# Attention of a hybrid encoder: products with v once per head over 512 queries, in place of twice over 256

## The chip, the cores and the metric

The kernel runs on one core of a Trainium2 chip. The metric is the device time of one execution in microseconds (us); a version's time is the median of its runs. A core has five engines that work side by side, each through its own queue in order: TensorE (PE in the profile; its weight loads are PEld), VectorE (DVE), ScalarE (ACT), GpSimd (POOL) and SyncE (SP, which here only issues DMAs). They wait for each other by semaphores.

## The reference

The model has two layers over 512 tokens of 1024 features in float32: a gated linear attention with a gated MLP, then a softmax attention with a second MLP. The change lies in the softmax attention. It has 8 query heads of 128 features; heads 0 to 3 share the first key and value head, 4 to 7 the second. Cut to what matters:

```python
def block(q_blk):                       # 128 queries
    s = jnp.einsum('bkgqd,bksd->bkgqs', q_blk, k).astype(jnp.float32) * scale
    p = jax.nn.softmax(s, axis=-1).astype(v.dtype)
    return jnp.einsum('bkgqs,bksd->bkgqd', p, v)

o = lax.map(block, qb)                  # 4 blocks of 128 queries
return o @ w_out                        # after the heads are put side by side
```

q and k have been normalised and rotated before. So each head gives, for each of its 512 queries, a row of 512 probabilities times v.

## The kernel before, in words

All products run in a reduced float32 form (fp32r). To keep the accuracy, each operand is split into a high part and a low part (the remainder), and each product is done as three: high by high, high by low, low by high (`mm3`, lines 266 to 268, which is where the profile puts them). A split is one copy on ScalarE (the high part) and one subtraction on VectorE (the low part).

The attention (`attention`, from line 640) first makes k, the first pair of q heads and v. `vh` and `vl` hold v, split, as four tiles of 128 tokens by 256 features. Then comes a loop that is written out by hand, over 32 blocks (8 heads times 4 blocks of 128 queries) and six steps more. Step t does, in this order of the program:

- `scores` of block t: three products of 512 columns into a PSUM bank "s" (two banks), the row maximum (`mx`, line 785), its scaling (`nb`, 786), and the exponential on ScalarE with the row sums (`p`, 788).
- what the plan gives for step t: steps of the q projections of the heads still to come (banks A and B, 24 products for each of the two banks, rotary products `rt` at line 679, splits of q), and from step 22 on steps of the output projection (`op`, line 321).
- `turn` of block t-4: four transposes of 128 x 128 into a bank "pt" (two banks, line 806), then the split of the transposed probabilities: `pth` (line 809, ScalarE) and `ptl` (line 810, VectorE), each 128 x 512.
- `shares` of block t: the reciprocal of the sum (`rc`, 793) and the scaling of p (794).
- `mix`, on every second step: the products with v for half a head (block t-6 and the one before). It takes four tiles of v times three products, each with 256 columns, the two blocks of queries, into one half of the bank "po" (one bank). After the second half the bank is split into oT (lines 705 and 706), which the output projection reads.

A half's transposed probabilities are one tile pair from the pool "g" (22 tiles), laid out as four key tiles by 256 queries. oT comes from "g" for heads 0 to 3 and from the pool "xhl" (8 tiles) for heads 4 to 7; "xhl" also holds the normalised input of the next MLP (`Norm.chunk`, lines 231 to 244), made in pairs of 128-feature chunks as the output projection ends. A scheduler orders the program's instructions for each engine by its own estimate of their times and keeps the program's order only where data demand it, so the order on each queue can shift when the program changes.

At the start, line 178 on, seven small float32 products on constants ("warm", each of which the profile records as two) run before the first data arrive. Their sum, -0.5, is copied to `halfneg` (line 184), the exponent of the reciprocal square roots later. The first real products are those of `vg` (line 295); their weights are the normalised x, their moving operand the first weights w_vg, split into `wh` and `wl`.

After the attention come the second MLP's up-products (`up`) and down-products (`dn`) with the same `mm3`.

Of the kernel before, what the change touches and what calls it, by code (L numbers as in the profile page):

```python
# [8 lines left out]
F32 = mybir.dt.float32  # L9
F32R = mybir.dt.float32r  # L10
U8 = mybir.dt.uint8
AF = mybir.ActivationFunctionType
ALU = mybir.AluOpType

P = 128
S = 512
D = 1024
KC = D // P
NT = S // P
# [27 lines left out]
def hybrid_encoder_kernel(  # L47
# [21 lines left out]
    pe, act, dve, pool, sync = nc.tensor, nc.scalar, nc.vector, nc.gpsimd, nc.sync  # L69
    mm = pe.matmul  # L70
# [7 lines left out]
    def nm(s):  # L78
        uid[0] += 1
        return f"{s}{uid[0]}"  # L80
# [3 lines left out]
    def bank(tag, n):  # L84
        return pp.tile([P, S], F32, tag=tag, bufs=PS[tag], name=nm(n))

    def pair(tag, bufs, dt, n):
        return sp.tile([P, 2 * S], dt, tag=tag, bufs=bufs, name=nm(n))

    def big(dt, n):  # L90
        return pair("g", 22, dt, n)

    def tmp(tag, n, w=S):
        return sp.tile([P, w], F32, tag=tag, bufs={"u": 4, "t": 6, "sq": 3}[tag], name=nm(n))
# [81 lines left out]

    two = tmp("u", "two")
    dve.memset(two[:, :P], 2.0 ** -5)
    dve.memset(two[:, P : 2 * P], -(2.0 ** -5))
    warm = bank("po", "warm")  # L180
    for i in range(7):
        mm(warm[:, :P], two[:, :P], two[:, P : 2 * P], start=i in (0, 3), stop=i in (2, 6))
    halfneg = cp.tile([P, 8], F32, name="halfneg")
    dve.tensor_copy(halfneg, warm[:, :8])
    ones = cp.tile([P, 1], F32, name="ones")
# [78 lines left out]
    def mm3(ps, wh, wl, mh, ml, start, stop):  # L264

        mm(ps, wh, mh, start=start, stop=False)  # L266
        mm(ps, wh, ml, start=False, stop=False)  # L267
        mm(ps, wl, mh, start=False, stop=stop)  # L268
# [371 lines left out]
    def attention(norm, nxt):  # L640
# [63 lines left out]
        def split(y, tile_):  # L704
            act.activation(tile_[:, :S], y, AF.Copy)
            dve.tensor_tensor(tile_[:, S:], y, tile_[:, :S].bitcast(F32), ALU.subtract)

        def whole(gen):
            while True:
                try:  # L710
                    next(gen)
                except StopIteration as e:
                    return e.value
# [52 lines left out]
        vh, vl = big(F32R, "vh"), big(F32R, "vl")  # L766
# [4 lines left out]
                                     ALU.mult, ALU.subtract)  # L771

        oh = [None] * QH
        probs, pts, pos = {}, {}, {}

        def scores(h, j):

            qt, sc, e = heads[h]
            kt = kk[h // 4]
            js = slice(j * P, (j + 1) * P)  # L780
            s = bank("s", "s")
            mm3(s, qt[:, js], qt[:, S + j * P : S + (j + 1) * P], kt[:, :S], kt[:, S:], True, True)
            scj = sc[:, 2 * j + e : 2 * j + e + 1]
            mx, nb, sm, rc = (tiny(1, n) for n in ("mx", "nb", "sm", "rc"))
            dve.reduce_max(mx, s, axis=mybir.AxisListType.X)
            dve.tensor_scalar(nb, mx, scj, -1.0, ALU.mult, ALU.mult)
            p = tmp("t", "p")
            act.activation(p, s, AF.Exp, scale=scj, bias=nb, accum_out=sm)
            probs[h, j] = (p, sm, rc)

        def shares(h, j):
            p, sm, rc = probs[h, j]
            dve.reciprocal(rc, sm)
            dve.tensor_scalar(p, p, rc, None, ALU.mult)
            probs[h, j] = p

        def turn(h, j):

            hf, i = divmod(j, 2)
            if i == 0:  # L800
                pts[h, hf] = tuple(big(F32R, n).rearrange("p (k q) -> p k q", q=256) for n in ("pth", "ptl"))
            ph3, pl3 = pts[h, hf]
            p = probs.pop((h, j))
            tp = bank("pt", "pt")
            for k in range(NT):
                pe.transpose(tp[:, k * P : (k + 1) * P], p[:, k * P : (k + 1) * P], ident)  # L806
            isl = slice(i * P, (i + 1) * P)
            tp3 = tp.rearrange("p (k q) -> p k q", q=P)
            act.activation(ph3[:, :, isl], tp3, AF.Copy)
            dve.tensor_tensor(pl3[:, :, isl], tp3, ph3[:, :, isl].bitcast(F32), ALU.subtract)  # L810

        def mix(h, hf):
            ph3, pl3 = pts.pop((h, hf))
            vo = (h // 4) * HD
            if hf == 0:
                pos[h] = bank("po", "po")
            dst = pos[h][:, hf * 256 : (hf + 1) * 256]
            for k in range(NT):
                vsl = slice(k * 256 + vo, k * 256 + vo + HD)
                mm3(dst, vh[:, vsl], vl[:, vsl], ph3[:, k, :], pl3[:, k, :], k == 0, k == NT - 1)  # L820
            if hf == 1:
                t = big(F32R, "oT") if h < 4 else pair("xhl", 8, F32R, "oT")
                split(pos[h], t)
                oh[h] = (t[:, :S], t[:, S:])

        LAG, LAG2 = LAGS
        blocks = [(h, j) for h in range(QH) for j in range(NT)]
# [9 lines left out]
        for t in range(len(blocks) + LAG2):  # L837
            if t < len(blocks):
                scores(*blocks[t])
            for g in plan[t]:  # L840
                next(g, None)
            if LAG <= t < len(blocks) + LAG:
                turn(*blocks[t - LAG])
            if t < len(blocks):
                shares(*blocks[t])
            if t >= LAG2:
                h, j = blocks[t - LAG2]
                if j % 2 == 1:
                    mix(h, j // 2)
        whole(osteps)  # L850

    norms = [Norm(i) for i in range(4)]
    cw = gla(norms[0], norms[1])
    ffn(0, norms[1], cw, norms[2])
    attention(norms[2], norms[3])
    ffn(1, norms[3], cw, None)

# [80 lines left out]
```

## Time and profile before

| what | value |
|---|---|
| median of 3 runs | 1135.59 us (1135.55 to 1136.19) |
| the profiled execution | 1135.46 us, of which the span from first to last instruction 1133.7 us |
| instructions | 13002 |
| attention's blocks in the trace | scores of the first about 628 us, last product with v at 742.0 us |
| products with v (`po`) | 192 of 128 x 256, from 654.7 to 742.0 us |
| output projection after the last of them | to about 770 us |

The profile is of one execution. Busy time of an engine is the time in which one of its instructions runs; instructions of TensorE are pipelined and overlap, so that the distance from one start to the next tells more than a duration. "Idle before" names what ended the wait. A line such as `L810 DVE TENSOR_TENSOR ptl<-pt,pth` reads: line 810, on VectorE, writes ptl from pt and pth. The chain of waits follows the work that ended last back to its beginning.

### The profile page before, as it was taken

To read this page: it belongs to the slowest core of one execution; us is meant where nothing else is said; L and a number is where in the kernel's file an instruction comes from. 1 tells how busy PE (TensorE), PEld (TensorE's weight loads), DVE (VectorE), ACT (ScalarE), POOL (GpSimd) and SP (SyncE) were. 2 spreads that over 40 slices of the span, in tenths; PEclk is the share of its full clock that TensorE was granted. 3 is DMA by queue.
4 is the path that set the end of the run, shared out by engine and by line. 5 is a ranking of instruction groups with operands and counts; after the bars stand their busy time and mean duration, and the time that the engine had idled before them with its cause. 6 is when DMAs were issued, how large, how long until landed. Compare 5 with 4: busy or idle time off the path is not lost.

```text
span 1133.7 us, 13002 instructions
## 1 busy us (share of the span) xinstructions
PE 1126.6 (99%) x5264; PEld 939.0 (83%) x5264; DVE 684.5 (60%) x988; ACT 481.5 (42%) x690; POOL 86.0 (8%) x74
## 2 busy tenths in 40 slices
PE   9999999999999999999999999999999999999998
PEld 7878888888888888888888888888888888888887
DVE  6576653577776777633325688766777677762221
ACT  6555233444444444422234667644444444442210
POOL 0214110000000000000004333000000000000000
PEclk9999999999999999999999999999999999999999
DMA  6322221232323223223247633223232232323320
GB/s 230 127 96 75 75 75 38 75 107 79 112 78 109 107 80 112 80 106 112 75 138 196 150 76 75 56 75 110 76 112 78 108 109 78 112 83 123 130 93 19
DMA packets 19980, 111.66 MB, mean 98 GB/s; under 512 B 2384, under 2 KB 3024, under 8 KB 8400
## 3 DMA queue, kind: packets, MB, share of 16 engines
q1 hardware_dynamic: 17328, 102.29, 25.7%
q0 software_dynamic: 2304, 8.39, 3.9%
q8 instruction: 41, 0.67, 0.2%
q10 hardware_dynamic: 288, 0.15, 0.0%
q14 instruction: 19, 0.16, 0.0%
HBM read 100.34 MB, written 2.10 MB: 90 GB/s over the span
## 4 chain that ended last, share of the span: by engine, by line
PE 94%; DVE 3%; ACT 2%; POOL 1%; issue 1%; DMA 0%; DVEq 0%; POOLq 0%; ACTq 0%
PE up L267 14%; PE up L266 14%; PE up L268 14%; PE op L321 8%; PE dn L266 7%; PE dn L267 7%; PE dn L268 7%; PE vg L295 3%; PE o L546 2%; PE pt L806 1%; PE av L295 1%; PE kv L522 1%; PE A L266 1%; PE A L268 1%; PE A L267 1%; PE B L266 1%
## 5 line engine op out<-in xcount | busy, mean ns | idle before, releaser
L143 ACT ACTIVATE wh<-raw 128x1024 fp32r<-128x1024 f32 x164 | 172.9, 1056 | 338.0 <-PE up L267 132.8
L144 DVE TENSOR_TENSOR wl<-raw,wh 128x1024 fp32r<-128x1024 f32 x164 | 203.8, 1243 | 142.7 <-ACT wh L143 142.4
L266 PE MATMUL up<-xhl,wh 128*128 128x512 f32 x704 | 274.3, 390 | 0.0
L268 PE MATMUL up<-xhl,wl 128*128 128x512 f32 x704 | 273.9, 389 | 0.0
L267 PE MATMUL up<-xhl,wh 128*128 128x512 f32 x704 | 273.9, 389 | 0.0
L266 PEld LDWEIGHTS up<-xhl,wh 128*128 128x128 f32 x704 | 132.2, 188 | 27.5
L268 PEld LDWEIGHTS up<-xhl,wl 128*128 128x128 f32 x704 | 132.2, 188 | 27.4
L267 PEld LDWEIGHTS up<-xhl,wh 128*128 128x128 f32 x704 | 132.2, 188 | 27.2
L267 PE MATMUL dn<-gu,wh 128*128 128x512 f32 x354 | 137.3, 388 | 0.0
L268 PE MATMUL dn<-gu,wl 128*128 128x512 f32 x354 | 137.3, 388 | 0.0
L266 PE MATMUL dn<-gu,wh 128*128 128x512 f32 x354 | 137.3, 388 | 0.0
L601 DVE TENSOR_TENSOR u<-up,R 128x512 f32<-128x512 f32 x88 | 60.3, 688 | 52.7 <-PE up L268 52.7
L295 PE MATMUL vg<-wh,xhl 128*128 128x512 f32 x256 | 80.1, 391 | 1.4 <-DVE g L364 0.5
L603 ACT ACTIVATE y<-u,cw 128x512 f32<-128x512 f32 x88 | 71.1, 811 | 20.4 <-DVE u L601 20.4
L268 PEld LDWEIGHTS dn<-gu,wl 128*128 128x128 f32 x354 | 66.5, 188 | 13.7
L266 PEld LDWEIGHTS dn<-gu,wh 128*128 128x128 f32 x354 | 66.5, 188 | 13.7
L267 PEld LDWEIGHTS dn<-gu,wh 128*128 128x128 f32 x354 | 66.5, 188 | 13.5
L321 PE MATMUL op<-oT,wh 128*128 128x512 f32 x256 | 70.8, 395 | 0.0
L605 DVE SCALAR_TENSOR_TENSOR y<-u,cw,y 128x511 f32<-128x511 f32 x88 | 65.9, 751 | 2.9
L604 DVE SCALAR_TENSOR_TENSOR y<-u,cw,y 128x511 f32<-128x511 f32 x88 | 65.5, 746 | 0.6 <-ACT y L603 0.6
L607 ACT ACTIVATE y<-y 128x512 f32<-128x512 f32 x44 | 27.9, 634 | 87.8 <-DVE y L605 87.7
L295 PEld LDWEIGHTS vg<-wh,xhl 128*128 128x128 f32 x256 | 47.9, 188 | 12.4 <-DVE g L364 0.9
(186 smaller groups left out, 1436.4 us busy)
## 6 DMA issues: line engine op xcount, KB each, us to landing
raw<-in_w_up_dram SPq DMA_DIRECT2D x44, 1024.0 KB, 4.8
raw<-in_w_down_dram SPq DMA_DIRECT2D x22, 1024.0 KB, 4.8
wl<-raw POOLq DMA_DIRECT2D x16, 512.0 KB, 4.8
raw<-in_w_vg_dram SPq DMA_DIRECT2D x6, 1024.0 KB, 4.8
raw<-in_w_akq_dram SPq DMA_DIRECT2D x5, 1024.0 KB, 4.9
raw<-in_w_kq_dram SPq DMA_DIRECT2D x4, 1024.0 KB, 4.8
raw<-in_w_gout_dram SPq DMA_DIRECT2D x4, 1024.0 KB, 4.7
raw<-in_w_aout_dram SPq DMA_DIRECT2D x4, 1024.0 KB, 4.7
```

Of the source, the lines that this page charges most:

```text
L143: act.activation(hi[:, sl], r[:, sl], AF.Copy)
L144: dve.tensor_tensor(lo[:, sl], r[:, sl], hi[:, sl].bitcast(F32), ALU.subtract)
L266: mm(ps, wh, mh, start=start, stop=False)
L267: mm(ps, wh, ml, start=False, stop=False)
L268: mm(ps, wl, mh, start=False, stop=stop)
L295: mm(ps[j][:, :width], hl[k][i == 2][:, js[j]], (wl if i == 1 else wh)[:, sl], start=k == 0 and i == 0, stop=k == KC - 1 and i == 2)
L321: mm(pss[ng][n], wt[:, sl], mv, start=k == 0 and i == 0, stop=k == KC - 1 and i == 2)
L601: dve.tensor_tensor(u, ps, norm.R, ALU.mult)
L603: act.activation(y, u, AF.Identity, scale=w(1), bias=w(3))
L604: dve.scalar_tensor_tensor(y[:, 1:], u[:, : S - 1], w(0), y[:, 1:], ALU.mult, ALU.add)
L605: dve.scalar_tensor_tensor(y[:, : S - 1], u[:, 1:], w(2), y[:, : S - 1], ALU.mult, ALU.add)
L607: act.activation(res[1], res[1], AF.Silu)
```

## The change

Three things change in the attention, and one at the start.

- `mix` runs once per head, at the step at which the second half ran, over all four blocks: 12 products of 512 columns in place of two times 12 of 256.
- For that, the transposed probabilities of a whole head are kept: two tile pairs, each two key tiles by 512 queries. `turn` now fills both pairs, so that it needs two copies and two subtractions of 128 x 256 in place of one of 128 x 512 each.
- oT comes from "g" for heads 0 to 2 and from "xhl" from head 3 on.
- The warm-up has eight products in one sum (16 records), with half the constant, so that the sum is still -0.5.

```diff
-    dve.memset(two[:, P : 2 * P], -(2.0 ** -5))
+    dve.memset(two[:, P : 2 * P], -(2.0 ** -6))
     warm = bank("po", "warm")
-    for i in range(7):
-        mm(warm[:, :P], two[:, :P], two[:, P : 2 * P], start=i in (0, 3), stop=i in (2, 6))
+    for i in range(8):
+        mm(warm[:, :P], two[:, :P], two[:, P : 2 * P], start=i == 0, stop=i == 7)
...
         def turn(h, j):
-            hf, i = divmod(j, 2)
-            if i == 0:
-                pts[h, hf] = tuple(big(F32R, n).rearrange("p (k q) -> p k q", q=256) for n in ("pth", "ptl"))
-            ph3, pl3 = pts[h, hf]
+            if j == 0:
+                pts[h] = [[big(F32R, n).rearrange("p (k q) -> p k q", q=S) for n in ("pth", "ptl")] for _ in range(2)]
...
-            isl = slice(i * P, (i + 1) * P)
             tp3 = tp.rearrange("p (k q) -> p k q", q=P)
-            act.activation(ph3[:, :, isl], tp3, AF.Copy)
-            dve.tensor_tensor(pl3[:, :, isl], tp3, ph3[:, :, isl].bitcast(F32), ALU.subtract)
-
-        def mix(h, hf):
-            ph3, pl3 = pts.pop((h, hf))
+            js = slice(j * P, (j + 1) * P)
+            for i, (ph3, pl3) in enumerate(pts[h]):
+                ks = slice(2 * i, 2 * i + 2)
+                act.activation(ph3[:, :, js], tp3[:, ks, :], AF.Copy)
+                dve.tensor_tensor(pl3[:, :, js], tp3[:, ks, :], ph3[:, :, js].bitcast(F32), ALU.subtract)
+
+        def mix(h):
             vo = (h // 4) * HD
-            if hf == 0:
-                pos[h] = bank("po", "po")
-            dst = pos[h][:, hf * 256 : (hf + 1) * 256]
+            po = bank("po", "po")
             for k in range(NT):
+                ph3, pl3 = pts[h][k // 2]
                 vsl = slice(k * 256 + vo, k * 256 + vo + HD)
-                mm3(dst, vh[:, vsl], vl[:, vsl], ph3[:, k, :], pl3[:, k, :], k == 0, k == NT - 1)
-            if hf == 1:
-                t = big(F32R, "oT") if h < 4 else pair("xhl", 8, F32R, "oT")
-                split(pos[h], t)
-                oh[h] = (t[:, :S], t[:, S:])
+                mm3(po, vh[:, vsl], vl[:, vsl], ph3[:, k % 2, :], pl3[:, k % 2, :], k == 0, k == NT - 1)
+            del pts[h]
+            t = big(F32R, "oT") if h < 3 else pair("xhl", 8, F32R, "oT")
+            split(po, t)
+            oh[h] = (t[:, :S], t[:, S:])
...
-                if j % 2 == 1:
-                    mix(h, j // 2)
+                if j == NT - 1:
+                    mix(h)
```

More of the change, by code (lines that the diff above doesn't have):

```diff
@@ L773, in attention @@
         oh = [None] * QH
-        probs, pts, pos = {}, {}, {}
+        probs, pts = {}, {}
         def scores(h, j):
```

## The prediction

> **What bounds the kernel now.** I read part 1 of the page first, then the busy time of the attention stage by stretch, then the waits, then the timelines of TensorE and VectorE inside the stage, and last the start of the program.
>
> ```profile
> PE 1126.6 (99%) x5264; PEld 939.0 (83%) x5264; DVE 684.5 (60%) x988; ACT 481.5 (42%) x690; POOL 86.0 (8%) x74
> ```
>
> TensorE is busy in nearly the whole span, so a microsecond of its work or of its waiting is a microsecond of the result. The share is an average, and the ends of products are modelled, so short waits can lie inside it. The stage that changes, by stretch (columns: length, then busy us of PE, PEld, DVE, ACT, POOL, the granted clock, DMA):
>
> ```profile
> 646.00:694.00 48.00, 48.00 (x286) 41.47 (x284) 38.88 (x89) 32.31 (x61) 16.68 (x13) 1.00 0.40 103
> 694.00:724.00 30.00, 29.74 (x184) 24.89 (x184) 26.51 (x64) 20.51 (x41) 8.78 (x7) 1.00 0.26 56
> 724.00:742.20 18.20, 18.20 (x113) 15.60 (x112) 9.13 (x19) 7.11 (x14) 0.00 (x0) 1.00 0.06 25
> ```
>
> From 646 to 694 us VectorE has 9 us of 48 free; from 694 to 724 it has 3.5 of 30. That second stretch decides. The waits from 700 to 728 us, and one step of VectorE's queue at 725 us:
>
> ```profile
> PEld s L266 <- ACT p L788: 1.7, 4, 0.7
> PE s L266 <- ACT p L788: 0.3, 1, 0.3
> ```
>
> ```profile
> 725.09 0.16 DVE L793 RECIPROCAL rc<-sm 128x1 f32<-128x1 f32 x1
> 725.17 0.67 DVE L785 TENSOR_REDUCE mx<-s 128x1 f32<-128x512 f32 x1
> 725.76 0.48 DVE L794 TENSOR_SCALAR p<-p,rc 128x512 f32<-128x512 f32 x1
> 726.15 0.21 DVE L786 TENSOR_SCALAR nb<-mx,qsc 128x1 f32<-128x1 f32 x1
> 726.28 0.68 DVE L810 TENSOR_TENSOR ptl<-pt,pth 128x512 fp32r<-128x512 f32 x1
> 727.36 0.16 DVE L793 RECIPROCAL rc<-sm 128x1 f32<-128x1 f32 x1 [0.40 <-ACT p L788]
> ```
>
> The scores of block t have two banks, so their weight load waits for the exponential of block t-2 (first fence). The second fence shows a ring that no engine can shorten: rc of a block, max of the next, p, nb, then the exponential on ScalarE, and rc again: 2.27 us per block (725.09 to 727.36), with ptl in the shadow of the exponential. In this stretch blocks follow each other every 2.67 us (exponential of block 20 at 699.40, of block 31 at 728.72): TensorE and this ring are nearly level.
>
> **The change part by part.** The built order of the changed kernel does what the diff says: 96 products of 512 columns in place of 192 of 256, two pth and two ptl per block in place of one.
>
> Products with v. Twelve of 256 columns start within 1.42 us (667.25 to 668.67), 0.118 each; those of 512 start every 0.23. 192 x 0.1183 - 96 x 0.23 = 22.7 - 22.1: **-0.6 us** of TensorE's own work. The Trainium skill ("TensorE: Matmul & The Clock Gate", section "Wait — 56ns, not 53.3ns?") has a fixed 2.5 ns per product, which would make it 96 x 2.5 ns = 0.24 us less work and the sum 1135.7; the rows give 7 ns a pair.
>
> Transposes. In the old order five groups of four are cut into 1 + 3 around the scores:
>
> ```profile
> 714.03 0.27 PE L806 MATMUL pt<-ident,p 128*128 128x128 f32 x1
> 714.25 0.50 PE L266 MATMUL s<-k,q 128*128 128x512 f32 x1
> 714.58 0.40 PE L267 MATMUL s<-k,q 128*128 128x512 f32 x1
> 714.81 0.39 PE L268 MATMUL s<-k,q 128*128 128x512 f32 x1
> ```
>
> One transpose and two score products take 0.78 us (714.03 to 714.81) where 0.11 + 2 x 0.23 = 0.57 would do. In the new order all groups stand whole: 5 x 0.2 = **-1.0 us**, if nothing else waits there. Open waits of the old order (two op products take 0.88 in place of 0.46 at 702.53; 0.2 more at 706 and 725) are worth another 0.6. TensorE by itself would so gain 2.2 us.
>
> Two evictions for one. The row of the whole, and the nearest rows of half its size from PSUM:
>
> ```profile
> L809 ACT ACTIVATE pth<-pt x32: 582/598/611, 646.7 to 736.8; 128x512 fp32r<-128x512 f32 x32
> L810 DVE TENSOR_TENSOR ptl<-pt,pth x32: 675/688/693, 647.3 to 738.1; 128x512 fp32r<-128x512 f32 x32
> ```
>
> ```profile
> L523 ACT ACTIVATE sa<-kv 128x256 f32<-128x256 f32 x8 | 3.1, 383 | 8.3 <-PE kv L522 8.3
> L636 DVE TENSOR_TENSOR x<-x,dn 128x256 f32<-128x256 f32 x2 | 0.8, 418 | 13.7 <-PE dn L268 13.7
> ```
>
> Two halves take 0.77 on ScalarE (+0.17) and 0.84 on VectorE (+0.15): 32 blocks make +5.4 and +4.8 us. As VectorE starts its next instruction 0.08 before the last one's end (max: 0.67 long, next after 0.59), a half holds the queue 0.34. Up to 694 us (blocks 0 to 18) the 9 free us of VectorE and 16 of ScalarE hide it; without that cover it would be the 2 us that 14 blocks bring. The sum of TensorE's work to the scores of block 19 is 0.27 lower.
>
> After that the order matters. In VectorE's new queue, from block 21 on, the second ptl half of a block four earlier stands **between max and nb**, in the ring: rc, mx, ptl half, p, nb; the first half stands in the shadow. The ring becomes 2.27 + 0.34 = **2.61 us**. The bounds: 2.27 if that half falls in time that p or nb would have waited for anyway, 2.95 if both halves come to lie in the ring. I take 2.61, since the order is fixed and the row of L636 has source and size. The Trainium skill ("VectorE: DVE Perf Modes", section "The DRAIN you can't avoid") says that the next instruction starts only when the pipe is empty, though one that is not held starts earlier; by the strict reading the half would cost 0.42, the ring 2.69 and the sum 1135.9. The rows show the overlap of 0.08.
>
> Now the walk. Scores of block 20 stand one us of TensorE's work earlier in the new order (fewer op products ahead), and the exponential of block 20 starts about 1.0 us earlier, at 698.4. On the next three steps VectorE has, besides the ring, a rotary product (0.66), a split of oT ahead of nb of block 22 (0.6) and one of q (0.6): the exponential of block 23 comes at 707.4 against 707.57. Eight ring steps of 2.61 bring that of block 31 to 728.3 (728.72 before), and that of block 29 to 723.1, ending 0.98 later, which frees the scores of block 31 at 724.1; they started at 725.11. TensorE is 1.0 ahead. From there to the last product with v stand 17.56 us of products in the new order (the mix of head 6 is whole there); the old took 17.05. One wait is new: transposes of block 28 need the bank of block 26, whose second half is subtracted behind max of block 31, at 727.8; TensorE is there at 727.5: +0.3. So 724.1 + 17.56 + 0.3 = 741.96 against 742.16: **-0.2 us**. The tail (oT of head 7 split while the products of head 6 run, 1.4 us of cover for 1.3) stays.
>
> Behind it, oT of head 3 now lives in an xhl slot, so the next norm's chunk 3 waits for its last reader, the fourth row of the last output group, about 764 us; it is needed as the fourth weight of the up-products, near 771.5, and 1.5 us of eviction fit: nothing. SP's queue is unchanged in the new order, POOL's puts the two rotary differences of one pair of heads ahead of its two sums, which need the later products: nothing.
>
> Warm-up: the start.
>
> ```profile
> 1.26 3.36 PE L182 MATMUL warm<-two 128*128 128x128 f32 x14 [1.26 <-DVE bd L188]
> 5.12 1.17 PE L295 MATMUL vg<-wh,xhl 128*128 128x512 f32 x4 [0.49 <-ACT sq L240]
> ```
>
> Two more records of 0.24 us end at 5.1 in place of 4.62, in the gap before 5.12. halfneg's copy (4.89) moves to 5.2 and pushes the first wl to about 6.0, read at 6.12: 0, at worst +0.3.
>
> Sum: 1133.7 of span and 1.76 around it are 1135.46, less 0.2: **1135.3**. The median of the three runs is 0.13 above the profiled one; the sum is not corrected for that.
>
> **Rivals.** *TensorE alone decides* (the ring stays at 2.27, or the new order lets TensorE run past it): -0.6 - 1.0 - 0.6 = 2.2 less, 1133.2. For it: TensorE at 99%, and blocks are 2.67 apart where the ring needs 2.27. Against it: scores waited for exponentials four times in this stretch already.
>
> *The ring decides, and is longer.* If the first half too slips out of the shadow (nb to rc is 1.2 us; a half and a split of oT or q fill 1.06 of it), a step takes 2.95 and eight steps bring 8 x 0.34 = 2.7 more: 1138.0, slower. It decides from 2.64 a step on (parity) and passes 0.2% at 2.9. For it: VectorE at 88% with 1.0 us more to do by 712. Against it: 0.1 us of the shadow is left.
>
> *The change buys and costs nothing here* because the scheduler undid it: excluded by the built order.
>
> **How the numbers follow.** 0.2% (2.3 us) is about what a measurement of this kernel can tell from no change. Forecast, ring at 2.55 to 2.85: 1134.8 to 1137.2 and the start's 0.3; chance 0.68. TensorE alone: 0.12, faster by just 0.2%. Longer ring: 0.20. The range goes to both rivals' values, 1133.2 to 1138.0, since the unknown is one price, the half's place in the ring, and it has those ends; half of either rival's chance lies beyond. Faster 0.12, same 0.68, slower 0.20.
>
> **What would show it.** In the changed profile: products with v start every 0.23; pth and ptl have 64 rows of about 0.38 and 0.42; rc to rc between blocks 23 and 30 is 2.6; the scores start right behind the accumulator read of the exponential two blocks before; last product with v near 742.0; first vg product still at 5.1. If rc to rc is 2.3, the first rival holds; at 2.9, the second. A wait before 694, or a gap between 764 and 775 us, would show a cover that I took for granted.

## The result, and the profile after

| | before | after |
|---|---|---|
| median | 1135.83 us (1135.55 to 1136.19, 7 runs) | 1139.33 us (1139.24 to 1139.78, 7 runs) |
| ratio | | 1.0028, 95% interval 1.0018 to 1.0037 |
| span of the profiled execution | 1133.7 us | 1137.5 us |

The change makes the kernel 0.3% slower: 3.5 us by the medians, 3.8 by the spans. The forecast was 1135.3, and the range to 1138.0 does not hold the result. In the experiments below, the runs of the kernel before fall into two groups some 1.5 us apart (beside experiments 7, 8, 9 and 12: 1135.3 to 1136.3 and 1137.2 to 1138.1 us), so that differences under a microsecond are not read from times alone but from the traces.

Part 1 of the page, and the busy time by stretch (length, then busy us of PE, PEld, DVE, ACT, POOL, granted clock, DMA), of the changed kernel:

```profile
PE 1128.7 (99%) x5170; PEld 934.5 (82%) x5170; DVE 687.9 (60%) x1020; ACT 484.7 (43%) x722; POOL 85.8 (8%) x74
```

```profile
646.00:694.00 48.00, 47.36 (x240) 38.59 (x240) 39.47 (x101) 32.59 (x72) 17.11 (x14) 1.00 0.39 101
694.00:724.00 30.00, 28.60 (x140) 20.89 (x139) 25.65 (x68) 20.10 (x49) 8.56 (x7) 1.00 0.28 70
724.00:742.00 18.00, 17.52 (x90) 14.05 (x89) 11.91 (x33) 10.01 (x25) 0.00 (x0) 1.00 0.01 2
```

The first line hides the loss: TensorE is still "99%" of the span. The stretches show it: from 694 to 724 us TensorE has 140 products in place of 184. Some of that is products twice as wide; but its idle time there went from 0.26 to 1.40 us, while VectorE, at 86%, was busy for less of the 30 us than before. TensorE's waits from 700 to 728 us:

```profile
PEld s L266 <- ACT p L788: 2.9, 6, 0.6
PEld pt L804 <- PE s L268: 1.3, 4, 0.4
PEld po L266 <- issue: 0.9, 1, 0.9
PE s L266 <- ACT p L788: 0.9, 4, 0.3
```

The scores now wait more for the exponential of two blocks earlier (2.9 us of weight loads in six waits, against 1.7 in four). To find where the time goes, I cut the attention at five starts on TensorE: the first scores, the scores of blocks 20, 24 and 31, and the last product with v. In us, each from the profile of that kernel (experiments are told below):

| kernel | to block 20 | 20 to 24 | 24 to 31 | 31 to last v | sum |
|---|---|---|---|---|---|
| before | 66.37 | 12.71 | 18.34 | 16.93 | 114.35 |
| **after** | 66.50 | 14.48 | 18.68 | 18.03 | **117.69** |
| old, halves only | 68.58 | 11.68 | 17.59 | 17.39 | 115.24 |
| old, whole-head mix of 256 columns | 66.69 | 13.34 | 16.99 | 17.74 | 114.76 |
| new, one copy | 66.40 | 13.13 | 17.29 | 16.79 | 113.61 |
| new, no GpSimd at the last pair | 66.49 | 12.93 | 18.72 | 18.05 | 116.19 |
| new, GpSimd beside p (experiment 7) | 66.50 | 14.50 | 22.23 | 19.35 | 122.58 |
| new, halves behind nb | 65.36 | 12.84 | 17.30 | 18.52 | 114.02 |
| new, rc and p late | 65.67 | 13.24 | 16.58 | 18.27 | 113.76 |
| old, rc and p late | 66.64 | 12.24 | 16.51 | 18.33 | 113.72 |
| new, p on ScalarE | 65.87 | 11.79 | 17.76 | 17.56 | 112.98 |

The stage grew by 3.34 us: 0.13 + 1.77 + 0.34 + 1.10. The remainder of the 3.8 is 0.39 ahead of the first scores and 0.07 behind the last product with v. The prediction had -1.0 to block 20, nothing from there to block 31, and +0.8 behind it.

But for the width of the products with v, the sums hold the same work; the single stretches need not, since the order of the output products differs. From block 24 to 31 TensorE has 22 output products and 36 of 256 columns with v before, and 12 and 23 of 512 columns after. That is the width of five products of 512 less, an estimated 1.1 us at 0.226 us each, so the +0.34 there hides some 1.5 us of new waiting. Behind block 31 it is the other way round.

Now the step of VectorE's queue that was shown of before at 725 us, in the changed kernel:

```profile
725.12 0.17 DVE L793 RECIPROCAL rc<-sm 128x1 f32<-128x1 f32 x1 [0.60 <-ACT p L788]
725.20 0.67 DVE L785 TENSOR_REDUCE mx<-s 128x1 f32<-128x512 f32 x1
725.79 0.42 DVE L810 TENSOR_TENSOR ptl<-pt,pth 128x256 fp32r<-128x256 f32 x1
726.12 0.48 DVE L794 TENSOR_SCALAR p<-p,rc 128x512 f32<-128x512 f32 x1
726.51 0.21 DVE L786 TENSOR_SCALAR nb<-mx,qsc 128x1 f32<-128x1 f32 x1
726.64 0.41 DVE L810 TENSOR_TENSOR ptl<-pt,pth 128x256 fp32r<-128x256 f32 x1
726.97 0.68 DVE L706 TENSOR_TENSOR oT<-po,oT 128x512 fp32r<-128x512 f32 x1
727.72 0.16 DVE L793 RECIPROCAL rc<-sm 128x1 f32<-128x1 f32 x1
```

The half of ptl stands between max and p, as foreseen; p starts 0.33 later behind max (726.12 against 725.79), and rc to rc is 2.60 where it was 2.27. But eight and seven steps earlier p itself looks different. The rows of p, pth and ptl (ns shortest/median/longest), then the two longest p and what GpSimd did at the time:

```profile
L794 DVE TENSOR_SCALAR p<-p,rc x32: 472/478/1560, 634.1 to 733.1; 128x512 f32<-128x512 f32 x32
L809 ACT ACTIVATE pth<-pt x64: 368/384/405, 647.1 to 742.7; 128x256 fp32r<-128x256 f32 x64
L810 DVE TENSOR_TENSOR ptl<-pt,pth x64: 405/415/426, 647.5 to 743.1; 128x256 fp32r<-128x256 f32 x64
```

```profile
702.18 1.43 DVE L794 TENSOR_SCALAR p<-p,rc 128x512 f32<-128x512 f32 x1
...
705.83 1.56 DVE L794 TENSOR_SCALAR p<-p,rc 128x512 f32<-128x512 f32 x1
```

```profile
700.68 2.63 POOL L698 TENSOR_TENSOR ry<-rt,rt 64x512 f32<-64x512 f32 x2 [0.73 <-DVE rt L679]
704.47 2.64 POOL L699 TENSOR_TENSOR ry<-rt,rt 64x512 f32<-64x512 f32 x2 [1.15 <-DVE rt L679]
```

A p scaling takes 0.48 us. These two take three times that, and they end at 703.61 and 707.39, which is 0.30 and 0.28 behind the ends of GpSimd's pairs of rotary operations (703.31 and 707.11). Both stand in the ring. The trace of before has the same, smaller:

```profile
701.14 1.13 DVE L794 TENSOR_SCALAR p<-p,rc 128x512 f32<-128x512 f32 x1
```

```profile
700.70 1.28 POOL L699 TENSOR_TENSOR ry<-rt,rt 64x512 f32<-64x512 f32 x1 [0.38 <-DVE rc L793]
```

Its p ends at 702.27, 0.29 behind the GpSimd operation's 701.98.

### The profile page after: what moved, and what is told of

It is laid out like the page before. It is cut to its first block, busy times and chain, and to the rows that moved or that the text cites. A ratio compares the mean times of both kernels' runs of the same rounds, so it can differ in the third digit from the quotient of the medians.

```text
span 1137.5 us, 12900 instructions
## 1 busy us (share of the span) xinstructions
PE 1128.7 (99%) x5170; PEld 934.5 (82%) x5170; DVE 687.9 (60%) x1020; ACT 484.7 (43%) x722; POOL 85.8 (8%) x74
## 4 chain that ended last, share of the span: by engine, by line
PE 90%; DVE 6%; ACT 2%; issue 1%; POOL 1%; DVEq 0%; POOLq 0%; ACTq 0%
PE up L266 14%; PE up L268 14%; PE up L267 14%; PE op L321 7%; PE dn L268 7%; PE dn L266 7%; PE dn L267 7%; PE vg L295 3%; PE o L546 2%; PE av L295 1%; PE kv L522 1%; DVE p L794 1%; DVE ptl L810 1%; DVE mx L785 1%; DVE wl L144 1%
```

## The experiments

**The theory.** Splitting the eviction of the transposed probabilities is the loss. Its halves stand in VectorE's queue inside the ring (rc, max, p, nb, exponential), so that the ring and no longer TensorE sets the pace, and the shifted order lets two p scalings start just as GpSimd begins work that they must wait for. **Rivals:** the longer warm-up; the mix in one lump per head; ScalarE or TensorE as the bound of these blocks.

Each kernel was compared with the kernel before on the same chip; ratios are given with their 95% intervals. Where a time is set against the changed kernel's 1139.3, the two were measured at different times and the difference is rougher. In the code, "..." marks lines left out.

**1. The changed kernel with the old warm-up**, seven products in two sums.

```diff
-    for i in range(8):
-        mm(warm[:, :P], two[:, :P], two[:, P : 2 * P], start=i == 0, stop=i == 7)
+    for i in range(7):
+        mm(warm[:, :P], two[:, :P], two[:, P : 2 * P], start=i in (0, 3), stop=i in (2, 6))
```

> The changed kernel with the old warm-up (seven products, 14 records). Theory 'start': the changed kernel's first four products with w_vg took 1.56 us (5.06 to 6.62) where they had taken 1.00 (5.12 to 6.12), because they ran before the clock was released or before the low part of w_vg came; with the old warm-up they start at 5.1 and end at 6.1 again and the run is 0.4 us faster than the changed kernel: 1138.9. Rival 'chance of one profile': the first products differ from run to run and not by the warm-up; the time stays at 1139.3.

Measured: 1139.0 us, ratio 1.0032 (1.0019 to 1.0044). The loss stays, and the stage is 117.69 us long, as in the changed kernel. The warm-up is not the cause of it; whether it costs the 0.4 us of theory 'start', the times do not tell.

**2. The kernel before with only the new warm-up** (the same edit the other way round).

> The kernel before, with nothing changed but the warm-up (16 records for 14). Theory A (the longer warm-up costs the start 0.4 us, as the changed kernel's first four vg products, 1.56 us in place of 1.00, would have it): those four take about 1.56 again, and the time is 0.4 above before. Theory B (those four products fall in a half-clock stretch or not from run to run, whatever the warm-up: 1.00 and 1.68 have both been seen with 14 records): time within 0.3 of before, the four products either 1.0 or 1.6.

Measured: 1136.18 against 1135.95, ratio 0.9998 (0.9989 to 1.0007); the stage 114.36. No cost that the times can tell. The first four products took 1.84 us here; the last section comes back to them.

**3. The kernel before with the split evictions only**: two copies and two subtractions of 128 x 256 into the old tiles, products with v as before.

```diff
-            act.activation(ph3[:, :, isl], tp3, AF.Copy)
-            dve.tensor_tensor(pl3[:, :, isl], tp3, ph3[:, :, isl].bitcast(F32), ALU.subtract)
+            for ks in (slice(0, 2), slice(2, 4)):
+                act.activation(ph3[:, ks, isl], tp3[:, ks, :], AF.Copy)
+                dve.tensor_tensor(pl3[:, ks, isl], tp3[:, ks, :], ph3[:, ks, isl].bitcast(F32), ALU.subtract)
```

> The kernel before with one part of the change alone: each transposed block is copied and subtracted in two halves of 128 x 256, into the same tile as before; the products with v stay at 256 columns, twice per head. Theory 'ring' (the halves lengthen VectorE's and ScalarE's work and the ring from one block's exponential to the next): most of the loss comes with this alone, 1138 to 1139, with a ring of 2.6 us in blocks 20 to 31. Rival 'lump' (the loss comes from making all products of a head at once, which starves VectorE of scores and then holds TensorE): 1135.8 to 1136.3.

Measured: 1136.98, ratio 1.0012 (1.0003 to 1.0021): 1.0 us slower, and not the 1138 to 1139 of theory 'ring'. Nor does the loss lie in the ring: between blocks 20 and 31 rc to rc is 2.27 to 2.84 and the two stretches are not longer than before. Its largest new wait comes earlier, where the copy of q stands later in ScalarE's queue (657.52 us, against 654.50 before):

```profile
658.22 0.50 PE L266 MATMUL s<-k,q 128*128 128x512 f32 x1 [0.69 <-ACT q L705]
```

These scores start 0.85 us later behind the product ahead of them than that product needs. Only two p scalings behind 651 us exceed 0.6 us, both 0.68. So the halves alone do not make the loss of 3.5 us; it takes the order that they get together with the product of a whole head.

**4. The kernel before with the mix of a whole head at once**, both halves of 256 columns at the step of the second, evictions unsplit.

```diff
-                t = big(F32R, "oT") if h < 4 else pair("xhl", 8, F32R, "oT")
+                t = big(F32R, "oT") if h < 3 else pair("xhl", 8, F32R, "oT")
...
-                if j % 2 == 1:
-                    mix(h, j // 2)
+                if j == NT - 1:
+                    mix(h, 0)
+                    mix(h, 1)
```

> The kernel before with the other part alone: all 24 products of 256 columns of a head are made together at the step of its last block, from four unsplit tiles; one copy and one subtraction per block stay, oT of head 3 is in xhl. Theory 'lump': 1138 to 1139.5. Theory 'ring': 1135.5 to 1136.3, since no instruction is added to VectorE.

Measured: 1135.89, ratio 0.9999 (0.999 to 1.0008). The lump costs nothing that the times can tell; the stage is 114.76 us, 0.4 longer.

**5. The changed kernel with one copy and one subtraction per block**: 512-column products, tiles filled in the old layout. The products read as much data as before but in another order, so that the attention's output is not the reference's.

```diff
...
-            for i, (ph3, pl3) in enumerate(pts[h]):
-                ks = slice(2 * i, 2 * i + 2)
-                act.activation(ph3[:, :, js], tp3[:, ks, :], AF.Copy)
-                dve.tensor_tensor(pl3[:, :, js], tp3[:, ks, :], ph3[:, :, js].bitcast(F32), ALU.subtract)
+            isl = slice(i * P, (i + 1) * P)
+            act.activation(ph3[:, :, isl], tp3, AF.Copy)
+            dve.tensor_tensor(pl3[:, :, isl], tp3, ph3[:, :, isl].bitcast(F32), ALU.subtract)
...
```

> The changed kernel with its 96 products of 512 columns once per head, but with the old single copy and subtraction per block into the old layout, so that the products read other columns than they should (the attention's output is not the reference's; every shape and count but the evictions is the changed kernel's). Theory 'ring': the loss goes and the 0.6 us of TensorE's work stay as a gain: 1135.0 to 1135.6 (0.4 of the start included). Theory 'lump': 1138 or more.

Measured: 1135.18, ratio 0.9992 (0.9983 to 1.0001); the stage is 113.61, 0.7 below before. rc to rc between blocks 27 and 31 is 2.25 to 2.38. With the split undone the whole loss goes, about 4 us against the changed kernel. A small gain of the wider products shows in the stage; the interval of the ratio does not tell it from none. The order moved too: the p scalings of blocks 20 and 21 took 0.84 and 0.47 us, so this kernel takes away the halves and most of GpSimd's hold at once.

**6. The changed kernel with more GpSimd work**, released by rc.

```diff
+            if 24 <= 4 * h + j < 31:
+                z = tmp("u", "z")
+                pool.tensor_tensor(z[0:64, :], cos[0:64, :], rc[0:64, :].to_broadcast([64, S]), ALU.mult)
```

> The changed kernel, with one more GpSimd operation (64x512, its result read by nobody) that starts with rc of each of blocks 24 to 30, beside the p scaling of that block. Theory A (a p scaling on VectorE is held while GpSimd works, as the 1.43 and 1.56 us at 702.18 and 705.83 suggest): p in these seven blocks takes 1.0 to 1.6 in place of 0.48, rc to rc goes from 2.57 to 3.1 to 3.6, and the time is 4 to 7 us above the changed kernel's 1139.3. Theory B (the two long scalings have another cause, and GpSimd's work does not touch VectorE's): p stays at 0.48, rc to rc at 2.57, time 1139.3.

Measured: 1140.12, ratio 1.0035 (1.0023 to 1.0048): 0.8 us more and not 4 to 7. The operation took 1.03 us and began 0.7 ahead of p, so only its last 0.34 fell beside p. p took 0.56 to 0.63 and again ended 0.29 behind it (716.55 against 716.26). The size was wrong, the direction right; so the timing was made sharper:

**7. The same, released by max**, so that the operation begins with p.

```diff
+            if 25 <= 4 * h + j < 32:
+                z = tmp("u", "z")
+                pool.tensor_tensor(z[0:64, :], cos[0:64, :], mx[0:64, :].to_broadcast([64, S]), ALU.mult)
```

> The changed kernel with one more GpSimd operation (64x512, 1.03 us, its result read by nobody) in each of blocks 25 to 31, released by max of the block, so that it starts some 0.1 us ahead of the p scaling of the block before. VectorE's and TensorE's orders are those of the changed kernel. Theory A (a p scaling does not end until some 0.3 us after the GpSimd operation beside it): p in these seven takes 1.1 to 1.25 in place of 0.48, rc to rc goes from 2.57 to 3.2 to 3.35, and the time is 4.5 to 5.5 us above 1139.3, some 1144.3. Theory B (GpSimd is not the cause of the long scalings): p 0.48, rc to rc 2.57, 1139.3.

Measured: 1144.29, ratio 1.0063 (1.005 to 1.0075). One pair of rows of this kernel:

```profile
716.05 1.22 DVE L797 TENSOR_SCALAR p<-p,rc 128x512 f32<-128x512 f32 x1
```

```profile
715.95 1.03 POOL L788 TENSOR_TENSOR z<-rope,mx 64x512 f32<-64x512 f32 x1 [0.75 <-issue]
```

p takes 1.15 to 1.22 in all seven, ending 0.29 behind GpSimd (717.27 against 716.98), and rc to rc is 3.20 to 3.34. Every number of theory A came out: seven p took 5.0 us more in all, and the kernel 5.0, so the ring carries a held p one for one into the time. Nothing on TensorE or ScalarE was changed.

**8. The changed kernel without GpSimd's four operations of the last pair of heads**.

```diff
             def head(e):
+                if i == 4 and keep == "qsc":
+                    return t[2 * e]
```

> The changed kernel without the four GpSimd operations of the last pair of heads (700 to 707 us; the q of these heads is then one rotary product, so the output differs). VectorE's and TensorE's orders are those of the changed kernel. Theory A (these operations hold two p scalings for 1.0 and 1.1 us, and the scores of block 24 come that much later): both take 0.48, the exponential of block 23 follows that of block 20 after 9.2 to 9.5 us in place of 11.4, and the time is 1.8 to 2.1 us below 1139.3, some 1137.3. Theory B (the ring alone makes the loss, and what blocks 20 to 23 lose would be waited for anyway): above 1138.5.

Measured: 1138.08, ratio 1.0011 (1.0002 to 1.002), where the changed kernel has 1.0028; its stage is 1.5 us shorter, all of it from block 20 to 24 (12.93 against 14.48). Both p are back at 0.48:

```profile
702.64 0.48 DVE L796 TENSOR_SCALAR p<-p,rc 128x512 f32<-128x512 f32 x1
```

```profile
705.46 0.48 DVE L796 TENSOR_SCALAR p<-p,rc 128x512 f32<-128x512 f32 x1
```

The exponential of block 23 follows that of block 20 after 9.67 us, not 11.36 (I expected 9.2 to 9.5). The time fell by 1.3 us where theory A had 1.8 to 2.1. GpSimd's work on the last pair thus costs the changed kernel about 1.5 us of its stage, and 1.8 us more than before remain without it. That is not quite the same as a share of the loss: the old kernel's p were held too, for 1.05 us in all against 2.03, and the old kernel without these operations was not run.

**9. The changed kernel with both halves of ptl behind nb.** The subtractions are held back to the next step and queued behind its nb.

```diff
...
+                late.append((pl3[:, :, js], tp3[:, ks, :], ph3[:, :, js].bitcast(F32)))
...
+                with tc.issue_after(nbi[0].ins):
+                    dve.tensor_tensor(*late.pop(0), ALU.subtract)
...
```

> The changed kernel with both halves of ptl put behind nb in VectorE's queue (rc, max, p, nb, ptl, ptl), so that none stands in the ring; the count and kind of instructions are the same. Theory A (the half between max and nb makes the ring 2.57): rc to rc between blocks 23 and 31 goes to 2.25 to 2.4 where no other split stands in it, and the time is 1.5 to 2.5 us below 1139.3. Theory B (TensorE or ScalarE sets the pace of these blocks): rc to rc stays near 2.55, and the time above 1138.8.

Measured: 1136.11, ratio 0.9994 (0.9985 to 1.0004). One step of its VectorE queue:

```profile
718.62 0.16 DVE L794 RECIPROCAL rc<-sm 128x1 f32<-128x1 f32 x1 [0.34 <-ACT p L789]
718.70 0.67 DVE L786 TENSOR_REDUCE mx<-s 128x1 f32<-128x512 f32 x1
719.29 0.48 DVE L795 TENSOR_SCALAR p<-p,rc 128x512 f32<-128x512 f32 x1
719.68 0.21 DVE L787 TENSOR_SCALAR nb<-mx,qsc 128x1 f32<-128x1 f32 x1
719.81 0.74 DVE L818 TENSOR_TENSOR ptl<-pt,pth 128x256 fp32r<-128x256 f32 x2
720.83 0.16 DVE L794 RECIPROCAL rc<-sm 128x1 f32<-128x1 f32 x1 [0.28 <-ACT p L789]
```

The ring is 2.21 us (718.62 to 720.83), with both halves in the shadow of the exponential; behind block 23 a step takes longer, 3.0 and 3.3, only where a split of oT stands ahead of nb. The same instructions, in another order, bring the kernel back to the old time. The gain exceeds the 1.5 to 2.5 that the ring alone was to give, as two more things moved: the way to block 20 is 1.1 us shorter, and GpSimd's operations alternate again as in the old kernel, so that they hold p for less (1.14 and 0.80 us). The scheduler also put some output products and ScalarE copies elsewhere, so the whole kernel does not isolate the ring. The stretch from block 24 to 31 comes nearest: TensorE has the same width of products there in both kernels (11 for the output and 24 with v, against 12 and 23), no p is held in either, and it takes 17.30 us in place of 18.68.

**10 and 11. rc and p one step later**, behind nb of the next block, in the changed kernel and in the old one: rc then waits for an exponential two blocks back, and the ring is open.

```diff
...
-            if t < len(blocks):
-                shares(*blocks[t])
+            if 1 <= t <= len(blocks):
+                with tc.issue_after(nbi[0].ins) if t < len(blocks) else ExitStack():
+                    shares(*blocks[t - 1])
```

> The changed kernel, with rc and p of a block issued one step later, behind nb of the next block: VectorE's queue has rc 21, max 23, p 21, a ptl half, nb 23, so rc waits for an exponential two blocks back and not for the last one. Theory A (the ring rc, max, p, nb, exponential sets the pace, and the halves of ptl in it make it late): the ring is gone, exponentials of blocks 20 to 31 follow each other every 2.3 to 2.6, and the time is 1134 to 1136.5. Theory B (only the two p scalings beside GpSimd's double operations cost): they are held as before, 702 and 706, and the time stays above 1138. Theory C (the transposes now wait, since p comes a step later): PE waits for p in the waits, 1137 or more.

> The kernel before with that same edit (rc and p one step later) and nothing else. If the ring binds in the old kernel too, between blocks 19 and 31, it becomes faster: 1133.5 to 1135. If TensorE sets the pace there (2.67 a block against a ring of 2.27), it stays within 0.5 of before.

Measured: the changed kernel 1135.64, ratio 0.9995 (0.9987 to 1.0004); the old one 1135.54, ratio 0.9997 (0.9988 to 1.0006). Opening the ring takes the loss away where the halves stand in it and does not change the time where they do not. In the old kernel's trace the stage is 0.6 us shorter (113.72), which is all that opening its ring brought: TensorE, by and large, sets the pace there, and in the changed kernel the ring did. With the ring open the two stages are level, 113.76 and 113.72. (The exponentials do not follow each other every 2.3 to 2.6 us, as theory A had it, but 1.3 to 5.1 us apart. The p of blocks 19 and 20 were held to 0.75 and 1.21 us, less than the 1.43 and 1.56 of the changed kernel, so part of the gain can be that.)

**12. The changed kernel with p scaled on ScalarE.**

```diff
-            dve.tensor_scalar(p, p, rc, None, ALU.mult)
+            act.activation(p, p, AF.Copy, scale=rc)
```

> The changed kernel with the p scaling on ScalarE (32 of some 0.58 us) in place of VectorE (0.48). It takes p out of VectorE's ring and out of GpSimd's way, and adds 0.58 to ScalarE's per block, which then has some 2.4 us a block (exponential 1.0, two pth 0.77, p 0.58). If VectorE's ring and the held scalings are the whole loss, the time is 1134 to 1136; if ScalarE then becomes the bound (a wait of p or of the transposes for it), 1137 or more.

Measured: 1134.65, ratio 0.998 (0.9971 to 0.9988): better than both kernels, 1.6 us below the median of before on the same chip and 0.6 below its fastest run. Its stretch from 694 to 724 us, and two rows of ScalarE:

```profile
694.00:724.00 30.00, 29.97 (x157) 23.73 (x156) 22.89 (x67) 28.48 (x69) 8.60 (x7) 1.00 0.19 36
```

```profile
720.49 0.78 ACT L788 ACTIVATE p<-s,nb,qsc 128x512 f32<-128x512 f32 x1
...
721.78 0.73 ACT L794 ACTIVATE p<-p,rc 128x512 f32<-128x512 f32 x1
```

TensorE is busy for 29.97 of the 30 us. p costs ScalarE 0.73 us (0.62 to the next start) and fills it to 28.48; yet no scores wait for an exponential by more than 0.4 us. The ring without p is 2.14 us even with the half in it, and none of the 32 p was held: they took 0.71 to 0.77 us. In this kernel the wider products come with a gain; the old kernel with p on ScalarE was not run, so how much of the gain is theirs is open.

## Why the prediction was wrong

The prediction had the ring and its length right, and still forecast a gain of 0.2 us. The step that failed most is its walk from block 20 to 23, where it put GpSimd's changed order at nothing; next come the cover that it took for granted up to block 20, and a tie between ring and TensorE that was none. Term by term:

- **TensorE as the bound, and the ring beside it**: borne out for the kernel before, whose time did not move with the ring open (experiment 11). That no engine can shorten the ring does not hold, though: with p on ScalarE it was 2.14 us with a half of ptl still in it (experiment 12). The groups of four transposes all stand whole in the changed kernel, as foreseen.
- **Products of 512 columns, halves of 0.38 and 0.42**: right. The twelve of the last head start 0.226 apart (743.28 to 745.77), so that the gain was 1.0 rather than 0.6: 192 x 0.1183 - 96 x 0.226. By the fixed 2.5 ns a product of the Trainium skill ("TensorE: Matmul & The Clock Gate", section "Wait — 56ns, not 53.3ns?") the estimate would be 0.24; the trace stays with the rows.
- **The ring at 2.61 us**: right, 2.54 to 2.60 from block 23 on. The strict reading of "The DRAIN you can't avoid" ("VectorE: DVE Perf Modes" in the Trainium skill), 2.69, does not hold here. The second rival named the right side, but with the wrong ring: 2.95 was never seen outside blocks 20 to 23.
- **Up to block 20, one us gained: wrong.** I compared sums of busy time ("9 us of 48 free") and not the order. Two transposes wait for a half of ptl that stands behind a rotary product in the queue:

```profile
657.86 0.41 PE L804 MATMUL pt<-ident,p 128*128 128x128 f32 x2 [0.36 <-DVE ptl L810]
```

```profile
684.97 0.41 PE L804 MATMUL pt<-ident,p 128*128 128x128 f32 x2 [0.28 <-DVE ptl L810]
```

  Against the spacing of the products ahead of them they lose 0.53 and 0.43 us, 0.96 in all. With the halves behind nb, and the same products on TensorE up to block 20, that way is 65.36, one us below before, which is what the prediction had.
- **The three steps from block 20 to 23 in 9.0 us: wrong, and the step that failed most.** They took 11.36. Of the 2.4 too many, 1.7 go when GpSimd's work goes (experiment 8: 9.67). The prediction said of GpSimd's changed order "nothing". It looked at when GpSimd's results are needed, and not at what VectorE does while GpSimd works, though the trace of before had the row: p 1.13 at 701.14, beside a GpSimd operation. In the old order two p were held for 0.65 and 0.40 us more than their 0.48; in the new, for 0.95 and 1.08.
- **The Trainium skill had the rule** ("SBUF — State Buffer", section "Who interferes with whom"): VectorE and GpSimd share one pair of SBUF ports as an exclusive lock; a VectorE operation that uses both ports, which a `tensor_scalar` can, and a GpSimd operation do not overlap, and the one that starts second waits for the whole of the other. This case agrees: each held p ended 0.28 to 0.30 us behind the GpSimd operation that had started before it. The page also says that a VectorE operation with two SBUF inputs contends with a GpSimd operation that reads SBUF; the split of q, 0.68 us alone, took 1.23 at 651.40 and 1.61 at 679.56, both ending 0.55 to 0.56 behind a GpSimd operation. Max and ptl, which read PSUM (ptl has one of its two inputs there), kept their 0.67 and 0.41 beside GpSimd at 701.3 to 702.2.
- **Behind block 31: +0.8 foreseen, +1.10 measured**: nearly right, the whole mix of head 6 and a wait for a bank.
- **The start: 0, at worst +0.3.** 0.39 in the profile; not told apart from nothing in the times (experiments 1 and 2).
- **Eight ring steps against the old pace**: the reasoning that 2.61 ties with 2.67 was right for these steps taken alone (18.68 us for blocks 24 to 31 against 18.34), but it left out that TensorE itself had less to do there, an estimated 1.1 us. With the halves out of the ring they take 17.30. The change's own gain was lost inside a step that I had called level.

In sum, by the spans the forecast missed 4.0 us (3.8 more, where 0.2 less was forecast). Of these 1.1 lie between the first scores and block 20, 2.1 between blocks 20 and 31, of which 1.5 go when GpSimd's work on the last pair goes, 0.3 behind block 31, and 0.4 at the start, which the times do not confirm. How the remainder between 20 and 24 divides between the longer ring, the split of oT ahead of nb of block 22 and a ScalarE weight cast that waited 1.25 us for an output product (709.3 to 710.5) was not taken apart; each experiment that moved one of them moved others as well.

## What to carry to other kernels

Where one engine's queue holds a ring of dependent steps, cutting an instruction in two is paid by where the second half comes to stand, not by the sum of busy time: write the new order of that queue down and walk it. Look in the rows of the ring's instructions for the longest beside the median; a 1.13 against 0.48 can point to a second engine that holds the ring, and that engine's timeline at the same moment shows whether it does. When a wider product needs two evictions in place of one, put both behind the ring's steps (experiment 9), or move other work off that engine in the same change (experiment 12).

## What the runs showed that I had not expected

A p scaling held by GpSimd shows in the profile as a long instruction, not as idle time, so that no view of waits names it: in the changed kernel p has no wait at all at 702.18 and 705.83, and VectorE counts as busy.

The first four products of the program take 1.00 us or 1.24 to 1.84 us, at the same granted clock of 1.00 in the profile. The changed kernel's rows:

```profile
5.06 1.72 PE L295 MATMUL vg<-wh,xhl 128*128 128x512 f32 x4
6.62 0.63 PE L295 MATMUL vg<-wl,xhl 128*128 128x512 f32 x2
```

From 5.06 to 6.62 four products start 0.39 apart; in the kernel before they start 0.25 apart (5.12 to 6.12). With the old warm-up four of five profiles showed about 1.00 and one 1.68; with the new one eight of nine showed 1.24 to 1.84 and one 1.01. That leans to a cost of the longer warm-up of about half a microsecond, which the comparison of times (0.9998, 0.9989 to 1.0007) neither shows nor excludes. In the slowest of these profiles (experiment 2) three steps in a row from one start to the next are 0.42 to 0.43 us, nearly twice the 0.23 of later products. Why they are slow was not found.
